# Attention regrouped into two kinds of visits, and a new order of the seven products, in a hybrid Mamba-2 and attention layer

## The chip, the cores and the metric

The kernel runs on one core of one Trainium2 chip. The metric is device time in microseconds of one execution. The reference for the change is the median of three runs of the kernel before. One more execution was recorded by the hardware profiler; every line of a profile below comes from it.

## What is computed

One decoder layer on x of 1024 tokens by 1024 channels, float32. The normed input goes through one large projection (9248 columns), which feeds two branches: a chunked state-space scan (Mamba-2) and a causal attention with 16 heads of 64 and a forgetting term. Both are multiplied by gates, projected, merged, projected once more, normed and added to x. Cut to what matters here:

```python
h = rmsnorm(x, pre_g)
z_ssm, xbc, dt_raw, q, k, v, f_raw, z_att, g_ssm, g_att = split(h @ w_in)
y = ssd(silu(conv(xbc)), softplus(dt_raw + dt_bias), a, d_skip)
y_ssm = group_rmsnorm(y * silu(z_ssm)) * ssm_norm_g
# attention, in blocks of 128 queries, for each head
s = q @ k.T / 8 + fcum[query] - fcum[key]          # fcum = cumsum(log sigmoid(f))
o = softmax(where(key <= query, s, -inf)) @ v
y_att = o * silu(z_att)
merged = sigmoid(g_ssm) * (y_ssm @ w_branch_ssm) + sigmoid(g_att) * (y_att @ w_branch_att)
out = x + rmsnorm(merged @ w_out, post_g)
```

## The kernel before

**Products.** Every large projection is done for a pair of 128-column units at a time (class `Pair`, line 281) by a scheme of Strassen's kind with seven products in place of eight, numbered 1 to 7. A product is 12 matmuls of 128x128 weights by 512 columns: four blocks of the inner dimension, each as high times high, high times low and low times high part, since the operands are split into a rounded part and the rest (`Pair.split` for the weights, tiles `wop`, lines 310 and 311; `Operands.split` for the columns, tiles `x0h`, `x0l` and so on, lines 248 to 252). The product numbers have these column operands: 1 `x0` (b11), 2 `x1` (b21), 6 `x4` (-t2), 5 `x3` (t1), 7 `x5` (t3), 4 `x6` (t4), 3 `x2` (-b22). Products 1, 6, 7 and 4 of a pair add up in one PSUM bank (`pb`). Between two of them ACT copies the sum so far (`keep`, line 358), and the next one must not start before that copy is done. 5 and then 3 use bank `pc`, 2 uses `pd` (or `pc` in attention). `give` (line 361) hands a finished quarter to its consumer, on DVE or, for product 4, ACT. There are 48 pairs.

**The order of the products** is written out by hand in `Stream.__init__` (line 412), as a list of steps. `Stream.half` issues half a product (6 matmuls); the weights of a step are made ready (`prepare`) three steps ahead. Other work is put between half products: `beside` for the scan, `fill` for attention. `halves` (line 533) stops early behind product 7 in attention, because product 4 would have to wait there for the copy of the common bank. Small work for later stages (`chores`: differences of operands on POOL, their stores) is taken off a list, one piece a half product.

**Attention** (from line 1225) runs for 8 pairs of heads, each in 6 groups (`GROUPS`, line 1247). A group is two blocks of 128 queries against up to 512 keys. The loop (line 1542) makes 96 half-visits and 3 more. Each does, in the order of PE's program: `weighted` (weighted sums of v, bank `av`) for what was turned in the half-visit before; `turned` (PE transposes of the exponentials `ex` into banks `pt`, and copies of these to `p` on ACT, line 1429) for half of the group before; `scores` of one query block for two heads (banks `s`, six matmuls on half the rows each, and four small bf16 matmuls `far` on a block that touches the diagonal), then the minimum on DVE (line 1409) and the exp on ACT (line 1412); then half products. Banks `s` and `pt` share four buffers. At the end of two groups, `settle`, `scale` and `send` turn the sums' reciprocals (`tp`, then `st_dram`), `take` loads them back spread over rows (`rb`), `gate` and `out` multiply on POOL, `free` copies `av` to `o` on ACT. Tiles `o` and `zr` have two buffers each.

**Queues.** Each engine does its instructions in order; those marked `pin` keep the program's order, others may be moved by the scheduler. Most DMAs are issued on SP's queue, also in order.

**The end of attention.** The last pair of heads has its output stored to `ya_dram`; its difference t4 is stored too; both are loaded again as `x1l` and `x6l` and split. Products 2 and 4 of the pair `ends[4]` need them. Pair `ends[4]` starts with 5, 6, 7, 2, then 1 of the next pair.

Of the kernel before, what the change touches and what calls it, by code (L numbers as in the profile page):

```python
# [16 lines left out]
P = 128  # L17
# [5 lines left out]
HALF = 512  # L23
# [63 lines left out]
def hybrid_layer(ctx: ExitStack, tc, a, out):  # L87
# [73 lines left out]
    class Operands:  # L161
# [82 lines left out]
        def split(self, name, j):  # L244
            h, l = (t[:, j, :] for t in self.tiles[name])
            raw = l.bitcast(F32)
# [6 lines left out]
            self.left[name].remove(j)  # L253

# [26 lines left out]
    class Pair:  # L281
# [7 lines left out]
        def __init__(self, keys, handlers, ops=None, adds=nc.vector):  # L289
            self.keys, self.handlers = keys, handlers  # L290
            self.ops = xop if ops is None else ops
            self.adds = adds
            self.raw, self.op, self.prepared = {}, {}, set()
            self.s1 = None
# [24 lines left out]
        def prepare(self, which):  # L319
# [15 lines left out]
            elif which == 7:  # L335
                self.split(7, self.total(r["a11"], r["a21"]))
# [38 lines left out]
        def do(self, which):  # L375
            if which in (2, 7, 4, 3):
                unit, ch = {2: (0, 0), 7: (1, 1), 4: (1, 0), 3: (0, 1)}[which]
                for begin in self.handlers[unit][2:]:
                    begin(ch)
            if which == 1:  # L380
                self.b = self.bank.tile([P, HALF], F32, tag="b", bufs=1, name="pb")
                yield from self.matmuls(self.b, 1, "b11", True)
                self.k1 = self.keep(self.b)
            elif which == 2:
                tag = "c" if self.alone else "d"
                ps = pj.tile([P, HALF], F32, tag=tag, bufs=1, name="p" + tag)
# [5 lines left out]
            elif which == 5:  # L392
                self.c = pj.tile([P, HALF], F32, tag="c", bufs=1, name="pc")
                yield from self.matmuls(self.c, 5, "t1", True)
# [10 lines left out]
    class Stream:  # L405
# [6 lines left out]
        def __init__(self, pairs, double, last):  # L412
            self.pairs = pairs
            for n, p in enumerate(pairs):
                p.bank = pjx if n < double and n % 2 else pj
# [18 lines left out]
            self.single = pairs[double : last + 1]  # L434
            for p in pairs:
                p.alone = p in self.single[:-1]
# [788 lines left out]
    with tc.tile_pool(name="att", bufs=1, reuse_waits="tile", side="right") as ap, tc.tile_pool(  # L1225
# [23 lines left out]
        SLOTS = [((2, 3), (0, 1)), ((0, 2), (1, 3)), ((0,), (2,)), ((1, 3), (0, 2)), ((0, 1), (2, 3)), ((0,), (1,))]  # L1249
        ex = ap.tile([P, 2, 4, 256], F32, name="ex")  # L1250
# [21 lines left out]
        class Heads:  # L1272
# [44 lines left out]
            def send(self, n):  # L1317

                tp = pj.tile([P, HALF], F32, tag="d", bufs=1, name="tp")
# [38 lines left out]
            def out(self, n):  # L1358
# [5 lines left out]
                elif self.last:  # L1364
                    nc.vector.tensor_tensor(z, self.av[n], z, ALU.mult)
# [7 lines left out]
        def scores(hp, g, u):  # L1373
# [22 lines left out]
            slots = SLOTS[g][u]  # L1396
            hd = heads[hp]
            for e in range(2):
                def shaped(ap_):
                    return ap_.rearrange("p (a c) -> p a c", c=256) if w == HALF else ap_  # L1400

                if len(slots) == 1:
                    o = ex[:, e, slots[0], 0:w]
                elif w == HALF:
                    o = ex[:, e, slots[0] : slots[1] + 1 : slots[1] - slots[0], :]
                else:
                    o = ex[:, e, slots[0] : slots[1] + 1, :].rearrange("p a c -> p (a c)")[:, 0:w]
# [226 lines left out]
```

## Time and profile before

| what | value |
|---|---|
| median of three runs | 1359.46 us (1355.67 to 1360.33) |
| the profiled execution | 1363.59 us |
| its span, first to last instruction | 1361.8 us |
| granted TensorE clock, mean | 0.993 |
| PE, PEld busy | 96%, 72% of the span |
| DVE, ACT, POOL busy | 72%, 60%, 25% |
| HBM traffic | 170 GB/s over the span |

How to read it: PE is TensorE's matmuls, PEld its loads of weights, which run beside them. DVE is VectorE, ACT ScalarE, POOL GpSimd, SP SyncE. A row of the timeline is: start in us, duration in us, engine, line and operation, output tile and inputs, sizes, and behind "x" how many instructions follow each other; in brackets idle time before it and what ended it. A row of the waits is: who waited for whom, total us, times, longest us. Matmuls are pipelined, their ends are modelled, and a row's duration reaches beyond the start of the next one; the distance between starts is what an instruction takes.

### The profile page before, as it was taken

The page shows a single profiled execution, that of the slowest core. Times are in us where ns is not written, and L with a number is a line of the kernel's source. Part 1 is how long each engine was busy: PE and PEld are TensorE (multiplying, and loading weights), DVE is VectorE, ACT ScalarE, POOL GpSimd, SP SyncE. Part 2 cuts the span into 40 slices and gives each one's busy share as a digit, 9 for nine tenths or more (in the row PEclk, how much of TensorE's full clock was granted, in tenths as well). Part 3 has the DMA queues.
Part 4 walks back from the last instruction along what each step waited for, and adds up shares of the span by engine and source line. Part 5 has one row for each costly group of instructions (what it writes and reads, how often), then busy time and mean ns, then how long its engine had stood idle before and what let it go on. Part 6 is the DMA issues. An engine that isn't in the chain of part 4 may idle for free. (4 is left out here: it accounts for less than half of the span.)

```text
span 1361.8 us, 21004 instructions
## 1 busy us (share of the span) xinstructions
PE 1302.9 (96%) x7070; PEld 980.0 (72%) x7070; DVE 979.0 (72%) x1852; ACT 822.5 (60%) x1773; POOL 336.6 (25%) x270
## 2 busy tenths in 40 slices
PE   5899999999999999999999999999899999889997
PEld 3578888787887888788776666676566665568776
DVE  7979886887878888887665555547655556766975
ACT  7645665566556656565556666668766467633654
POOL 3000440014201420041001223222132322346262
PEclk9999999999999999999999999999999999899989
DMA  7232543445445544444475556468756547576632
GB/s 282 72 108 67 172 133 129 148 151 158 148 142 159 153 138 144 149 134 128 151 244 161 177 178 197 155 213 286 247 179 194 192 144 260 191 235 195 238 102 100
DMA packets 153452, 229.92 MB, mean 169 GB/s; under 512 B 15456, under 2 KB 57920, under 8 KB 153344
## 3 DMA queue, kind: packets, MB, share of 16 engines
q1 hardware_dynamic: 146768, 217.33, 49.7%
q10 hardware_dynamic: 6432, 10.72, 2.1%
q8 instruction: 56, 0.92, 0.3%
q14 instruction: 52, 0.43, 0.1%
q0 software_dynamic: 144, 0.52, 0.1%
HBM read 161.16 MB, written 70.50 MB: 170 GB/s over the span
## 5 line engine op out<-in xcount | busy, mean ns | idle before, releaser
L311 DVE TENSOR_TENSOR wop<-sum,wop 128x512 fp32r<-128x512 f32 x192 | 151.7, 791 | 109.3 <-ACT wop L310 108.9
L310 ACT ACTIVATE wop<-sum 128x512 fp32r<-128x512 f32 x192 | 119.9, 626 | 85.7 <-DVE sum L316 32.1
L1412 ACT ACTIVATE ex<-ex,nm 128x512 f32<-128x512 f32 (+1 forms) x192 | 116.8, 610 | 84.7 <-DVE nm L1409 79.3
L358 ACT ACTIVATE s<-pb 128x512 f32<-128x512 f32 x144 | 85.2, 592 | 99.6 <-PE pb L130 96.5
L130 PE MATMUL pc<-x2h,wop 128*128 128x512 f32 x384 | 132.9, 405 | 6.7 <-DVE th L370 3.2
L130 PE MATMUL pb<-x4h,wop 128*128 128x512 f32 x384 | 130.4, 398 | 1.5 <-ACT x4h L248 1.5
L130 PE MATMUL pb<-x0h,wop 128*128 128x512 f32 x384 | 131.6, 401 | 0.0
L1409 DVE CUSTOM_DVE_ANT_0 ex<-s,fb 128x512 f32<-128x512 f32 (+1 forms) x192 | 99.4, 553 | 44.1 <-PE s L130 43.6
L130 PE MATMUL pc<-x3h,wop 128*128 128x512 f32 x384 | 129.4, 396 | 1.3 <-DVE th L372 1.3
L130 PE MATMUL pb<-x6h,wop 128*128 128x512 f32 x384 | 128.5, 395 | 1.4 <-ACT s L358 1.4
L130 PE MATMUL pb<-x5h,wop 128*128 128x512 f32 x384 | 129.0, 395 | 0.7 <-ACT s L358 0.7
L311 DVE TENSOR_TENSOR wop<-raw,wop 128x512 fp32r<-128x512 f32 x132 | 96.4, 731 | 25.2 <-ACT wop L310 23.5
L133 PE MATMUL pt<-ident,ex 128*128 128x128 f32 x576 | 87.5, 284 | 11.2 <-ACT ex L1412 9.2
L130 PE MATMUL pd<-x1h,wop 128*128 128x512 f32 x288 | 96.9, 395 | 0.6 <-ACT x1h L251 0.6
L310 ACT ACTIVATE wop<-raw 128x512 fp32r<-128x512 f32 x132 | 82.3, 624 | 19.4 <-PE pc L130 11.4
L133 PEld LDWEIGHTS pt<-ident,ex 128*128 128x128 f32 x576 | 61.0, 140 | 45.6 <-issue 20.1
L1429 ACT ACTIVATE p<-pt 128x512 f32<-128x512 f32 (+1 forms) x160 | 81.9, 548 | 18.4 <-PE pt L133 18.3
L130 PEld LDWEIGHTS pc<-x2h,wop 128*128 128x128 f32 x384 | 73.0, 190 | 27.2 <-DVE th L370 4.6
L316 DVE TENSOR_TENSOR sum<-raw 128x512 f32<-128x512 f32 x80 | 61.3, 766 | 42.7 <-DMA raw<-in_wu 31.3
L130 PEld LDWEIGHTS pb<-x4h,wop 128*128 128x128 f32 x384 | 72.9, 190 | 19.3 <-issue 2.0
L130 PEld LDWEIGHTS pb<-x0h,wop 128*128 128x128 f32 x384 | 73.5, 192 | 18.1 <-issue 2.5
L130 PEld LDWEIGHTS pc<-x3h,wop 128*128 128x128 f32 x384 | 72.1, 188 | 19.9 <-issue 2.9
(286 smaller groups left out, 2992.4 us busy)
## 6 DMA issues: line engine op xcount, KB each, us to landing
raw<-in_wu SPq DMA_DIRECT2D x128, 256.0 KB
csb<-cs_dram SPq DMA_DIRECT2D x32, 256.0 KB
fb<-f_dram SPq DMA_DIRECT2D x16, 512.0 KB
rb<-st_dram SPq DMA_DIRECT2D x48, 128.0 KB
wd<-in_wo SPq DMA_DIRECT2D x40, 128.0 KB
xt<-in_x SPq DMA_DIRECT2D x8, 512.0 KB
gs_dram<-th ACTq DMA_DIRECT2D x16, 256.0 KB
qh_dram<-th SPq DMA_DIRECT2D x16, 256.0 KB
```

The source lines that it names most:

```text
L130: return tc.keep_in_program_order(nc.tensor.matmul(*args, **kw))
L133: return tc.keep_in_program_order(nc.tensor.transpose(out_, in_, idn))
L310: nc.scalar.activation(op[:, 0], src, AF.Copy)
L311: nc.vector.tensor_tensor(op[:, 1], src, op[:, 0], ALU.subtract)
L316: self.adds.tensor_tensor(t, x, y, ALU.add)
L358: nc.scalar.activation(s, ps, AF.Copy)
L1409: nc.vector.tensor_tensor_reduce(o, shaped(s[e][:, 0:w]), shaped(fb[hp, h][:, e, 0:w]), 1.0, 3.0e38, ALU.add, ALU.min, nm)
L1412: nc.scalar.activation(o, o, AF.Exp, scale=-1.0, bias=nm, accum_out=hd.at(hd.sm, i, h, e))
L1429: nc.scalar.activation(p[:, :, first:, :], bank[:, :, first:, :], AF.Copy)
```

## The change

Attention now has 48 visits. One does: `weighted` for all that the visit before turned; `scores` for both query blocks of a group; 0.68 of the share of products; `turned` for the whole group, its copies alternately on ACT and DVE; the other 0.32 of the products. The minimum and the exp are pinned. `ex` holds a group in a plain layout. `tp` is put in one of the four score banks. `o` and `zr` have one buffer each, `p` four. Loads are issued at other places of the loop. Where the last outputs of attention are made, `direct` makes the operands b21 and t4 from tiles in the chip's own memory, on DVE and ACT.

The order of the seven products in the main run is 6, 2, 7, 5, 1 of the next pair, 4, 3 (before: 2, 6, 5, 7, with 1 of the next pair behind 7 or, in attention, behind 3). Product 1's bank alternates between two for all pairs, also in attention; the early stop in `halves` is gone. Since 7 may stand before 5, the subtraction of the two follows whichever comes second. Product 7's sum of weights is made in place in the raw tile.

```diff
+        def direct(self, j, outputs, gates, x):
+            pin(nc.vector.tensor_tensor(gates, outputs, gates, ALU.mult))
+            pin(nc.vector.tensor_tensor(x, x, gates, ALU.subtract))
+            for name, raw in (("b21", gates), ("t4", x)):
+                self.at[name, j] = self.step
+                self.split(name, j, raw)
+            self.made.add(("t4", j))
...
             elif which == 7:
-                self.split(7, self.total(r["a11"], r["a21"]))
+                if self.keys[0][0] == "merged":
+                    self.split(7, self.total(r["a11"], r["a21"]))
+                else:
+                    self.adds.tensor_tensor(r["a11"], r["a11"], r["a21"], ALU.add)
+                    self.split(7, r["a11"])
...
-            elif which == 7:
-                yield from self.matmuls(self.b, 7, "t3", False)
-                self.give(1, 1, self.c, self.keep(self.b), "less")
+                else:
+                    yield from self.matmuls(self.b, 7, "t3", False)
+                    self.k7 = self.keep(self.b)
+                self.sums += 1
+                if self.sums == 2:
+                    self.give(1, 1, self.c, self.k7, "less")
...
-                p.bank = pjx if n < double and n % 2 else pj
+                p.bank, p.other = (pj, "be"[n % 2]), (pjx, "d") if n < double else (pj, "c")
...
-                early = [(nxt, 1)] if n + 1 < double else []
-                late = [(nxt, 1)] if n + 1 >= double else []
-                self.steps += [(p, 2), (p, 6), (p, 5), (p, 7)] + early + [(p, 4), (p, 3)] + late
+                self.steps += [(p, 6), (p, 2), (p, 7), (p, 5), (nxt, 1)]
+                self.steps += [(p, 4), (p, 3)] if n + 1 < last else [(p, 3), (p, 4)]
...
-            self.steps += [(a, 5), (a, 6), (a, 7), (a, 2), (b, 1), (a, 4), (a, 3)]
+            self.steps += [(a, 5), (a, 6), (a, 7), (b, 1), (a, 2), (a, 4), (a, 3)]
...
-                if self.run is None and self.at and self.at < len(self.steps):
-                    p, which = self.steps[self.at - 1]
-                    if which == 7 and p in self.single:
-                        return
...
-                tp = pj.tile([P, HALF], F32, tag="d", bufs=1, name="tp")
+                tp = pp.tile([P, HALF], F32, tag="s", bufs=4, name="tp")
...
-                    self.zr = ap.tile([P, HALF], F32, tag="zr", bufs=2, name="zr")
+                    self.zr = ap.tile([P, HALF], F32, tag="zr", bufs=1, name="zr")
...
-                self.o[n] = ap.tile([P, HALF], F32, tag="o", bufs=2, name="o")
+                self.o[n] = ap.tile([P, HALF], F32, tag="o", bufs=1, name="o")
...
-                    nc.vector.tensor_tensor(z, self.av[n], z, ALU.mult)
+                    stream.do_chores()
+                    ops_a.direct(self.hp - KH, self.av[n], z, state["t"])
+                    attended.add((self.hp, 0))
+                    return
...
                 with tc.high_priority():
-                    nc.scalar.activation(p[:, :, first:, :], bank[:, :, first:, :], AF.Copy)
+                    if b % 2:
+                        nc.vector.tensor_copy(to, src)
+                    else:
+                        nc.scalar.activation(to, src, AF.Copy)
...
+        for m in range(6 * NK + 1):
+            last = m == 6 * NK
+            for hd, which in end(m - 2):
+                if (hd.last, which) != (True, 1):
+                    hd.gate(which)
+            for one in made:
+                weighted(*one)
+            for hd, which in end(m - 1):
+                if last:
+                    hd.gate(which)
+                    hd.out(which)
+                    break
+                hd.free(which)
+            if last:
+                break
+            hp, g = divmod(m, 6)
+            if not g:
+                heads[hp] = Heads(hp)
+            for u in range(2):
+                scores(hp, g, u)
+            for hd, which in end(m - 1):
+                (hd.take if (hd.last, which) == (True, 1) else hd.send)(which)
+            for hd, which in end(m):
+                hd.settle(which)
+            loads(m)
+            fill(m, 0.68)
+            for hd, which in end(m - 2):
+                if (hd.last, which) != (True, 1):
+                    hd.out(which)
+            for hd, which in end(m - 1):
+                if (hd.last, which) == (True, 1):
+                    hd.gate(which)
+                    hd.out(which)
+                else:
+                    hd.take(which)
+            for hd, which in end(m):
+                hd.load_gates(which)
+                hd.scale(which)
+            made = turned(hp, g)
+            for hd, which in end(m):
+                if hd.last and which:
+                    hd.send(which)
+            fill(m, 0.32)
+            if m == 6 * NK - 1:
+                heads[hp].take(2)
```

More of the change, by code (lines that the diff above doesn't have):

```diff
@@ L375, in do @@
         def do(self, which):
-            if which in (2, 7, 4, 3):
-                unit, ch = {2: (0, 0), 7: (1, 1), 4: (1, 0), 3: (0, 1)}[which]
+            if which in (2, 4, 3) or which in (5, 7) and self.sums:
+                unit, ch = {2: (0, 0), 4: (1, 0), 3: (0, 1)}.get(which, (1, 1))
                 for begin in self.handlers[unit][2:]:
@@ L1507, in begins @@
                     nc.sync.dma_start(state["t"], ops_a.block("t1", hp - KH))
-            if s == 9 and more:
-                load_v(hp + 1, 1)
-            if s == 10:
+            if g == 4:
                 if more:
@@ L1514, in begins, with end @@
                     state["y"] = fetched("b11", hp - KH)
-        def ended(n):
-            for back in range(6):
-                hp, s = divmod(n - back, 12)
-                if n >= back and hp < NK and s in (3, 7, 11):
-                    yield back, heads[hp], s // 4
+            if g == 5 and more:
+                load_k(hp + 1, 0)
+                load_q(hp + 1, (5, 4))
+        def end(m):
+            hp, g = divmod(m, 6)
+            if 0 <= hp < NK and g % 2:
+                yield heads[hp], g // 2
         load_q(0, (7, 6))
@@ L1532, in hybrid_layer, with fill @@
         weights = (1.1, 1.1, 1.1, 1.1, 0.75, 0.95, 1.05, 0.85)
-        left = [12 * sum(weights) + 3 * weights[-1]]
-        def fill(n):
-            share = weights[min(n // 12, NK - 1)]
+        left = [6 * sum(weights)]
+        def fill(m, part):
+            share = weights[min(m // 6, NK - 1)] * part
             to = stream.steps.index((ends[4], 6))
@@ L1541, in hybrid_layer @@
         made = []
[L1542 to L1572 removed]
+        for m in range(6 * NK + 1):
[13 more added lines that the diff above has]
+                break
+            hp, g = divmod(m, 6)
+            if not g:
[16 more added lines that the diff above has]
+                else:
+                    hd.take(which)
+            for hd, which in end(m):
[4 more added lines that the diff above has]
+                if hd.last and which:
@@ L1583, in hybrid_layer @@
     for n, p in enumerate(ends[4:]):
-        p.bank = pjx if n % 2 else pj
+        p.bank, p.other = ((pjx, "b") if n % 2 else (pj, "b")), (pjx, "d")
     while stream.half():
```

111 lines of the change are left out of this document (34 added, 77 removed).

## The prediction

> **What bounds the kernel now.** I read the page's head first: whose engine is full, and where the granted clock falls.
>
> ```profile
> span 1361.8 us, 21004 instructions
> PE 1302.9 (96%) x7070; PEld 980.0 (72%) x7070; DVE 979.0 (72%) x1852; ACT 822.5 (60%) x1773; POOL 336.6 (25%) x270
> PE   5899999999999999999999999999899999889997
> PEclk9999999999999999999999999999999999899989
> ```
>
> PE is busy in every slice but the first; DVE and ACT have room on the average. The table by stage says the same of each stage (columns: busy time of PE, PEld, DVE, ACT, POOL, then granted clock, DMA share, GB/s); the rows are the scan with its projections, the attention, the few microseconds in which attention ends, and the rest.
>
> ```profile
> 60.00:695.00 635.00, 626.49 (x3211) 506.82 (x3210) 513.09 (x860) 368.71 (x725) 119.72 (x116) 1.00 0.46 144
> 695.00:1179.00 484.00, 469.09 (x2977) 315.05 (x2975) 286.46 (x722) 324.40 (x798) 122.52 (x93) 1.00 0.61 198
> 1179.00:1207.00 28.00, 20.76 (x80) 14.45 (x81) 17.51 (x27) 11.77 (x23) 5.09 (x5) 0.88 0.68 218
> 1207.00:1361.00 154.00, 143.42 (x614) 116.34 (x614) 113.39 (x162) 73.81 (x148) 76.38 (x47) 0.97 0.49 167
> ```
>
> In the 484 us of attention PE idles 14.9 us. So removing waits there can give at most 15 us. But "busy" is not the same as "at its pace", since ends of matmuls are modelled: the distances between starts have to be read. First a product of twelve matmuls in the scan stage, from its first start to the next one's first:
>
> ```profile
> 402.44 0.39 PE L130 MATMUL pd<-x1h,wop 128*128 128x512 f32 x1
> 405.17 0.39 PE L130 MATMUL pb<-x4h,wop 128*128 128x512 f32 x1
> ```
>
> That is 2.73 us, 0.227 us a matmul of 512 columns. Now half-visits of attention, each of which does, in this order, av (weighted sums), pt (turnings), s (scores), products:
>
> ```profile
> 805.57 1.08 PE L130 MATMUL av<-p,v 128*64 128x256 f32 x8
> 806.58 1.09 PE L133 MATMUL pt<-ident,ex 128*128 128x128 f32 x8
> 807.61 0.79 PE L130 MATMUL s<-k,q 64*128 64x384 f32 x6
> ...
> 855.56 0.66 PE L133 MATMUL pt<-ident,ex 128*128 128x128 f32 x4
> 856.15 0.97 PE L130 MATMUL s<-k,q 64*128 64x512 f32 x6
> 857.05 0.50 PE L130 MATMUL pb<-x4h,wop 128*128 128x512 f32 x1
> 859.99 0.65 PE L130 MATMUL av<-p,v 128*64 128x256 f32 x4
> 860.57 0.44 PE L133 MATMUL pt<-ident,ex 128*128 128x128 f32 x2
> ```
>
> Eight turnings take 1.03 us to the next block, four take 0.59: 0.11 each, and 0.15 that does not depend on their number. Eight av matmuls take 1.01, four take 0.58: 0.15 fixed as well. Six score matmuls run as three pairs beside each other (two halves of the rows), 0.68 at the pace above, and take 0.90: 0.22 fixed. The product takes 2.94 instead of 2.73: 0.21 fixed. No wait stands in these rows. So **a half-visit pays 0.73 us for changing the kind of work**, a group of two half-visits 1.46, and 48 groups 70 us. This is the part of the time that the waits don't show.
>
> **The change, part by part.** *Grouping.* The order of PE's instructions in the changed kernel has 48 visits in place of 96: av of a whole group, both blocks of scores, a product part (12 matmuls in 36 visits, 18 in 12), all turnings of the group, 6 more product matmuls. Attention holds 936 product matmuls before and after, and 24 `tp`. Two of the five new boundaries have a row each:
>
> ```profile
> 700.10 0.50 PE L130 MATMUL pc<-x1h,wop 128*128 128x512 f32 x1
> 702.96 1.03 PE L133 MATMUL pt<-ident,ex 128*128 128x128 f32 x8
> ...
> 1188.88 0.44 PE L133 MATMUL pt<-ident,ex 128*128 128x128 f32 x2
> 1189.07 0.48 PE L130 MATMUL pb<-x0h,wop 128*128 128x512 f32 x1
> 1190.64 0.44 PE L130 MATMUL av<-p,v 128*64 128x128 f32 x4
> ```
>
> A product between scores and turnings: 2.86, 0.13 fixed. Turnings ahead of a product: two in 0.19 where the pace says 0.22, so -0.03. A half product between turnings and av: 1.57 against 1.36, 0.21 fixed. Scores ahead of a product: 0.22 as above. Av straight ahead of scores occurs nowhere in the trace; between nothing and the two fixed costs that it replaces (0.30) I take 0.15, that of av ahead of turnings, its nearest row. Sum 0.68 a group: 0.78 saved, times 48 = **-37 us**. Bounds: 45 saved with av to scores free; 18 if that costs 0.30 and the other four cost what their kinds cost above (0.21+0.15+0.21+0.22).
>
> *Second block of scores behind the first one's corner.* Where the block touches the diagonal (32 visits), bf16 corner matmuls now stand between two blocks of scores. Not in the trace: nothing to 0.15 each (the smallest fixed cost), 0 to 5 us. I take **+2**.
>
> *Waits at the turnings.* Most of PE's waits in attention are there already (the list from 695 to 1183: total, times, longest), and behind them stands the chain of DVE and ACT after one block of scores:
>
> ```profile
> PE pt L133 <- ACT ex L1412: 9.2, 14, 3.7
> PE pt L133 <- DVE nm L1409: 1.5, 1, 1.5
> ...
> 857.15 0.69 DVE L1409 CUSTOM_DVE_ANT_0 ex<-s,fb 128x512 f32<-128x512 f32 x1 [1.14 <-PE s L130]
> 857.88 0.72 ACT L1412 ACTIVATE ex<-ex,nm 128x512 f32<-128x512 f32 x1 [0.84 <-DVE nm L1409]
> 858.61 0.71 ACT L1412 ACTIVATE ex<-ex,nm 128x512 f32<-128x512 f32 x1
> 862.42 0.68 DVE L1409 CUSTOM_DVE_ANT_0 ex<-s,fb 128x512 f32<-128x512 f32 x1
> ```
>
> Scores began at 856.15: the minimum starts 1.00 later, the first exp 1.73, the next one 0.73 after that. Four exps, now pinned behind each other, end 4.65 us after the scores begin. PE in that time: two blocks of scores 1.58, a product 2.86, so turnings at 4.44, and the third, the first that reads the fourth exp, at 4.66. The cover is exactly enough where 12 matmuls stand before the turnings (36 visits), and 1.4 us too long where 18 do. Every delay of DVE or ACT ahead of the minima is then a wait of PE: the minimum at 862.42 starts 1.48 behind its scores (860.94, on PE), 0.48 late. I take 0.55 in 36 visits, 20 us, against the 15 that PE idles in the stage now: **+5**. Bounds: none, -15; one DVE and one ACT instruction in front each time (0.69 + 0.59, the copies below), 46 us, +31.
>
> *Turnings evacuated by two engines.* Eighty copies go from ACT to DVE, at about 0.69 us (a DVE subtraction out of the same banks):
>
> ```profile
> L1429 ACT ACTIVATE p<-pt 128x512 f32<-128x512 f32 x127 | 70.8, 591 | 14.7 <-PE pt L133 14.6
> L370 DVE TENSOR_TENSOR th<-pc,s 128x512 f32<-128x512 f32 x11 | 7.6, 692 | 20.0 <-ACT s L358 11.4 <-issue 8.6
> ```
>
> DVE in attention goes from 286 to about 340 us of 447, ACT from 324 to 277. The cover is the six product matmuls (1.57) between turnings and av; nothing counted beyond the delays above.
>
> *Product order and banks.* In the scan, PE idles 8.5 of 635 us; both orders leave a product between each copy of a bank and its next use, and weights are prepared three steps ahead as before. In attention the bank of product 1 now alternates, and 7 is no longer followed by 4 in one bank. Cost **0**, bounds -4 to +4 (half of the idle time there). `tp` in a score bank waits for the first minimum, which starts 1.0 us after the scores and ends at 1.7; `tp` stands at 1.58 or later: within the delays above.
>
> *The end of attention.* The waits from 1179 to 1210, and the clock behind the longest:
>
> ```profile
> PE tp L133 <- DVE ns L1307: 3.2, 1, 3.2
> PE pb L130 <- ACT x4h L248: 1.5, 1, 1.5
> PE pb L130 <- DVE x4l L249: 1.0, 1, 1.0
> PE pd L130 <- ACT x1h L251: 0.6, 1, 0.6
> ...
> 1183.11 0.37 PE L133 MATMUL tp<-ident,ns 128*8 128x128 f32 x1 [3.23 <-DVE ns L1307]
> 1183.71 0.63 PE L130 MATMUL pc<-x2l,wop 128*128 128x512 f32 x1
> 1184.14 1.06 PE L130 MATMUL pc<-x2h,wop 128*128 128x512 f32 x2
> ```
>
> After 3.23 us of idling, matmuls start 0.43 apart instead of 0.23, and the stage's granted clock is 0.88. The change sends the last sums behind the turnings, and `direct` makes the last operands of products 2 and 4 without a trip through memory, with product 1 of the next pair as cover. The waits of t2's parts (x4) stay. Of 6.3 us of waits and some 2 us of slow clock I take **-5**; bounds -9 and +3.
>
> **Sum:** -37 +2 +5 -5 = -35 us. The profiled execution took 1363.6 (span 1361.8); the median of the runs shown is 1359.5, 4.1 less. 1363.6 - 35 - 4.1 = **1324**.
>
> **The rivals.**
>
> *Waits eat the gain.* If the delay is 1.2 us in 36 visits (43 us): -37+2+28-5 = -12, so 1347. For it: no slack in the chain. Against: DVE and ACT now have one gap of several microseconds to catch up in, instead of two short ones.
>
> *Cover was generous.* No waits at the turnings and none at the end: -37-15-9 = -61, so 1298.
>
> *Slower: one buffer for `o` and `zr`.* ACT's copy of av into `o` now waits for POOL's last read of the one before. Now that takes:
>
> ```profile
> 829.64 0.27 PE L133 MATMUL tp<-ident,ns 128*8 128x128 f32 x1
> 838.13 1.28 POOL L1367 TENSOR_TENSOR zr<-o,zr 128x512 f32<-128x512 f32 x1
> ```
>
> From `tp` to POOL's end 9.8 us. In the changed kernel the next copy of `o` is two visits behind, 18 us or more at 9.3 us a visit. SP, too, stands at the load of `zr` until the output before it is stored, and `rb` is queued behind. If this makes POOL over 9 us later, ACT stops with the exps behind it, 23 times: at 3 us each 69 us, and -35+69 = +34, 1393; it is slower from 1.5 us each on. Against it: those 9 us of slack.
>
> *Slower through the clock.* If waits at the turnings pass the 3.2 us after which the pace halved, each costs about 2 us more (some ten matmuls at 0.20 each), 5.2 together, in place of the 0.55 in the sum. Ten such visits give -35+47 = +12, 1371; it is slower from eight on. The Trainium skill, "TensorE: Matmul & The Clock Gate", Parts 1 and 4, has a rule against this change: the clock halves after an idle window of about 3.4 us, and transposes do not count as activity in the same way. By that rule sixteen turnings in a row (1.8 us) plus a wait of 1.6 would do, three times the delay that I take; the trace so far has granted 1.00 in attention, with turnings in every half-visit.
>
> *It does not do what it says.* If the fixed costs move to the new boundaries at full price (18 saved), the second blocks cost 5, and DVE, at 76%, is late by 0.9 in 36 visits (32 us, +17): -18+5+17-5 = -1, 1358, no change.
>
> **How the numbers follow.** Chances: forecast 0.60 (own range 1308 to 1340), waits eat the gain 0.17, generous 0.08, `o` and `zr` 0.07, clock 0.03, not what it says 0.05. A measurement of this kernel can tell about 0.3%, 4 us. Faster: 0.60+0.17+0.08 = 0.85; same 0.05; slower 0.07+0.03 = 0.10. The range goes from 1304 (between forecast and generous) to 1354, which takes in the first rival and leaves out the last three and half of the generous one, some 0.19.
>
> **What would show it.** Steps: starts of av and of the block behind it, 1.0 us for eight and for sixteen about 1.9, must show one fixed cost a block; the stage from 695 to the last av (1191) shrinks from 496 to some 463; PE's waits for ACT's exp at the turnings near 20 us. Wrong if: those waits exceed 40 us, ACT's `o` waits for POOL, the granted clock in attention falls below 0.97, or the scan stage (60 to 695) gets longer by over 4 us.

## The result, and the profile after

The changed kernel takes 1374.59 us in the median of five runs (1368.88 to 1376.63), the kernel before 1360.33 beside it: ratio **1.0102, 95% interval 1.0071 to 1.0134**. It is 1% slower; 1324 was forecast, 35 us faster. The profiled execution took 1368.88, the shortest of the five, so its parts add up to some 5 us less than a usual run.

The head of the page after:

```profile
span 1367.2 us, 20913 instructions
...
PE 1278.0 (93%) x7070; PEld 996.2 (73%) x7070; DVE 1018.3 (74%) x1932; ACT 787.1 (58%) x1693; POOL 340.9 (25%) x270
...
PE   6899999999999999999999989999789997899997
```

PE is busy 25 us less than before and the whole is longer, so PE now waits where it was full. The stages, with the first and the last of attention's matmuls as borders (columns: busy time of PE, PEld, DVE, ACT, POOL, then granted clock, DMA share, GB/s):

```profile
60.00:710.00 650.00, 634.60 (x3232) 513.39 (x3231) 513.30 (x863) 371.91 (x728) 124.82 (x116) 0.99 0.44 140
710.00:1190.00 480.00, 436.74 (x2925) 324.33 (x2924) 317.10 (x791) 284.00 (x709) 121.85 (x94) 0.97 0.59 197
```

In attention PE now idles 43 of 480 us where it idled 15 of 484, and the granted clock is 0.97 where it was 1.00. From the starts of the instructions in both traces (waits are gaps of over 0.3 us on PE; at half clock half of the time is lost):

| | before | after |
|---|---|---|
| the scan's last product starts (no. 201 of 203 or 204) | 685.0 | 699.6 |
| first scores to last av | 495.8 | 492.1 |
| last av to the end | 170.7 | 164.5 |
| waits of PE: scan, attention | 7.7, 15.5 | 15.0, 41.4 |
| time at half clock: scan, attention | 0, 10.2 | 6.8, 27.3 |

One product of 2.7 us has moved from behind attention to ahead of it. So the scan lost 14.6 us where nothing was forecast; attention gained 3.7 instead of 33; its end gained 3.5 besides the moved product.

**The saving itself came.** One visit of the timeline, without waits:

```profile
750.07 0.48 PE L130 MATMUL pc<-x2h,wop 128*128 128x512 f32 x1
...
752.90 1.69 PE L133 MATMUL pt<-ident,ex 128*128 128x128 f32 x14
754.34 0.48 PE L130 MATMUL pb<-x4h,wop 128*128 128x512 f32 x1
...
755.91 1.74 PE L130 MATMUL av<-p,v 128*64 128x256 f32 x16
757.58 0.62 PE L130 MATMUL s<-k,q 64*128 64x256 f32 x6
```

From start to start: a product 2.83 (forecast 2.86), fourteen turnings 1.44, a half product 1.57 (as forecast), sixteen av, four of them with half the columns, 1.67: one fixed cost a block. If each kind of block is counted at the lower quartile of its times, the blocks of attention sum up to 470.8 us before and 436.3 after: **-34.5 us**, forecast -37 and +2. What lies above that sum was 25 us before and is 56 after, and eats the gain. It is in the waits (attention after; total, times, longest):

```profile
PE tp L133 <- DVE nm L1414: 21.0, 11, 4.5
PE pt L133 <- ACT ex L1418: 12.2, 12, 4.2
PE av L130 <- ACT p L1437: 4.6, 5, 1.5
PE tp L133 <- DVE ns L1325: 3.2, 1, 3.2
PE av L130 <- DVE p L1435: 2.2, 4, 1.5
```

The largest is not at the turnings, but at `tp`: it stands right behind the scores and takes the score bank that the first minimum must free. The longest of these places, PE first and then DVE:

```profile
1132.48 0.96 PE L130 MATMUL s<-k,q 64*128 64x512 f32 x6
...
1138.74 0.38 PE L133 MATMUL tp<-ident,ns 128*8 128x128 f32 x1 [4.47 <-DVE nm L1414]
1138.77 0.78 PE L130 MATMUL pc<-x2h,wop 128*128 128x512 f32 x1
1139.35 0.63 PE L130 MATMUL pc<-x2l,wop 128*128 128x512 f32 x1
```

```profile
1133.20 1.77 DVE L321 TENSOR_TENSOR wop<-raw,wop 128x512 fp32r<-128x512 f32 x1
1136.38 0.69 DVE L253 TENSOR_TENSOR x0l<-x0l,x0h 128x512 fp32r<-128x512 f32 x1 [1.42 <-ACT x0h L252]
1137.39 0.69 DVE L253 TENSOR_TENSOR x0l<-x0l,x0h 128x512 fp32r<-128x512 f32 x1 [0.31 <-ACT x0h L252]
1138.00 0.68 DVE L1414 CUSTOM_DVE_ANT_0 ex<-s,fb 128x512 f32<-128x512 f32 x1
```

The minimum could start 1.1 us after the scores, as in undisturbed visits, and starts 5.5 after them. Ahead of it in DVE's order stand a split of weights stretched to 1.77 us (.69 undisturbed) and two splits of operands that wait for ACT. Behind the wait the first two matmuls start 0.58 apart, where the pace is 0.23. In the 48 visits, 12 first minima start 1.9 us or more after their scores. Lateness as such is not new: in the kernel before, 21 of the 96 half-visits have such a first minimum, the longest 5.4 us behind its scores, and PE's waits at the turnings are 10.7 us in all; 15 are of the first block of a group, with the second half-visit, some 5 us, still between it and its turnings. What the change took away is that distance.

### The profile page after: what moved, and what is told of

The parts are those of the page before. It is cut to its first block, busy times and chain, and to the rows that moved or that the text cites. A ratio compares the mean times of both kernels' runs of the same rounds, so it can differ in the third digit from the quotient of the medians.

```text
span 1367.2 us, 20913 instructions
## 1 busy us (share of the span) xinstructions
PE 1278.0 (93%) x7070; PEld 996.2 (73%) x7070; DVE 1018.3 (74%) x1932; ACT 787.1 (58%) x1693; POOL 340.9 (25%) x270
## 5 line engine op out<-in xcount | busy, mean ns | idle before, releaser
L321 DVE TENSOR_TENSOR wop<-raw,wop 128x512 fp32r<-128x512 f32 x176 | 134.2, 763 | 39.1 <-ACT wop L320 38.6
L321 DVE TENSOR_TENSOR wop<-sum,wop 128x512 fp32r<-128x512 f32 x148 | 112.7, 762 | 53.2 <-ACT wop L320 52.8
L130 PE MATMUL pb<-x5h,wop 128*128 128x512 f32 x384 | 133.1, 405 | 3.1 <-ACT s L373 3.0
L320 ACT ACTIVATE wop<-sum 128x512 fp32r<-128x512 f32 x148 | 92.4, 626 | 66.0 <-PE pc L130 28.1
L1414 DVE CUSTOM_DVE_ANT_0 ex<-s,fb 128x512 f32<-128x512 f32 (+1 forms) x192 | 95.8, 552 | 46.2 <-PE s L130 46.2
L320 ACT ACTIVATE wop<-raw 128x512 fp32r<-128x512 f32 x176 | 109.4, 623 | 32.2 <-PE pd L130 21.7
L130 PEld LDWEIGHTS pb<-x5h,wop 128*128 128x128 f32 x384 | 74.2, 193 | 20.3 <-ACT s L373 4.8
L133 PE MATMUL pt<-ident,ex 128*128 128x128 f32 x576 | 76.9, 282 | 12.2 <-ACT ex L1418 12.2
L209 POOL TENSOR_TENSOR wd<-wd 128x256 f32<-128x256 f32 x32 | 33.2, 1038 | 209.4 <-DMA wd<-in_wo 193.9
L130 PEld LDWEIGHTS pb<-x4h,wop 128*128 128x128 f32 x384 | 72.8, 190 | 17.1 <-issue 1.5
L133 PEld LDWEIGHTS pt<-ident,ex 128*128 128x128 f32 x576 | 67.7, 145 | 23.6 <-ACT ex L1418 16.7
```

Of the source, the lines that this page charges most:

```text
L130: return tc.keep_in_program_order(nc.tensor.matmul(*args, **kw))
L133: return tc.keep_in_program_order(nc.tensor.transpose(out_, in_, idn))
L209: pin(nc.gpsimd.tensor_tensor(t[out_], t[a_], t[b_], ALU.subtract))
L320: nc.scalar.activation(op[:, 0], src, AF.Copy)
L321: nc.vector.tensor_tensor(op[:, 1], src, op[:, 0], ALU.subtract)
L1414: nc.vector.tensor_tensor_reduce(o, s[e][:, 0:w], fb[hp, h][:, e, 0:w], 1.0, 3.0e38, ALU.add, ALU.min, nm)
```

## The experiments

Theory A: attention's saving is real, but its cover (what PE does between scores and what needs them) has no slack, and DVE is late; waits and the clock behind them take it back. Theory B: the new order of the seven products costs the scan 12 to 15 us. Times are told as ratios to the kernel before on the same chip; .001 is 1.4 us. Beside each ratio is its interval.

### The scan: order and sum in place

**e1_old_scan_order** puts the scan's order back:

```diff
-                self.steps += [(p, 6), (p, 2), (p, 7), (p, 5), (nxt, 1)]
+                if n + 1 < double:
+                    self.steps += [(p, 2), (p, 6), (p, 5), (p, 7), (nxt, 1)]
+                else:
+                    self.steps += [(p, 6), (p, 2), (p, 7), (p, 5), (nxt, 1)]
```

> The changed kernel, with only the products of the scan stage put back to their order before (2, 6, 5, 7, next 1, 4, 3); attention as changed. In the changed kernel's profile the scan stage ends 14.6 us later than before with the same products. Theory B (the new order itself makes the scan's vectors late: operands that are due sooner, sums that come in another place): the scan stage gives 11 to 15 us back, about 1362 us beside 1375. Rival (the scan is late by the banks that now alternate, or by chance of where vector work falls, whatever the order): within 4 us of 1375, scan stage ends at 697 or later. By theory B attention, 492 us from the first scores to the last output product, stays within 6 us of that.

Measured 1.0065 (1.0041 to 1.0089), 5 us less than the change. The scan's last product starts at 690.5: 9 us are back, 5.5 are not. Neither theory's number; and the interval overlaps that of the change, so that the whole time alone does not show the gain.

**e2_before_new_order** is the opposite, the kernel before with the new order in the scan; since 7 then precedes 5, three sums would be alive at once in two buffers, so the sum for 7 is in place here too.

> The kernel before, with only the products of the scan stage in the new order (6, 2, 7, 5, next 1, 4, 3), the sum for product 7 formed in place as the change does, and the difference given after the second of 7 and 5. Theory B: the scan stage ends 10 to 15 us later than the 685 us of before, some 1372 us in all. Rival (the order is harmless, something else of the change lengthens the scan): within 4 us of 1360.

Measured 1.0187 (1.0159 to 1.0216), +25 us: the scan ends at 703.3 (+18), attention takes 6 more. The parts that concern the products cost more than the whole change does.

**e10_own_sum** is e1, and the sum for product 7 has its own buffer again wherever the order is the old one:

```diff
-                if self.keys[0][0] == "merged":
+                if self.keys[0][0] == "merged" or not self.inplace:
                     self.split(7, self.total(r["a11"], r["a21"]))
```

> The changed kernel with the scan's products in the order before (as in the run of that name, 1368.7 us), and there the sum for product 7 formed in a buffer of its own again, as before. In that run the scan still ended 5.5 us later than before, 1.9 us of it by product 6 and 3.2 at 160 us. If the sum in place is the cause (it holds a weights' buffer until the split, so the next weights come later): the scan gives 4 to 6 us back, 1363 to 1365. If the banks, or the place where products fall, are the cause: within 2 us of 1368.7.

Measured .9998 (.9978 to 1.0018): the scan's last product starts at 682.3, and all that the scan had lost is back, by the profiles 9 us through the order and 8 through the sum in place (by the ratios 5 and 9). The two together are sure, their shares less so: in the nine kernels profiled here that have the scan of the change, the first scores start at 707.0 to 714.7, in the six with the scan of e10 at 691.8 to 695.2. Not all of it reached the end in the profile: e10's attention takes 506.4 us there, 14 more than after, with 49.2 of waits and 44.4 at half clock, in an execution 3.7 us above its median. A place where the sum in place shows, e1's DVE first and then e10's:

```profile
162.82 0.69 DVE L326 TENSOR_TENSOR sum<-raw 128x512 f32<-128x512 f32 x1 [4.44 <-DMA raw<-in_wv]
163.43 0.68 DVE L806 TENSOR_TENSOR m<-m,cbm 128x512 f32<-128x512 f32 x1
```

```profile
156.47 1.10 DVE L807 TENSOR_TENSOR m<-m,cbm 128x512 f32<-128x512 f32 x1
159.33 0.69 DVE L326 TENSOR_TENSOR sum<-raw 128x512 f32<-128x512 f32 x1 [1.75 <-DMA raw<-in_wv]
```

In e1 the next pair's sum stands ahead of the scan's mask `m` on DVE and waits 4.44 us for weights; PE waits 1.99 for `m`, and runs at half clock after it. In e10 the sum stands behind `m`. So two things differ here, when the load lands and where the sum stands in DVE's order; their shares of the 8 us were not separated. Who holds back the weights' loads is seen on SP's queue, after and then before:

```profile
SPq L313 <- DVE wop L321: 50.9, 23, 7.8
...
SPq L313 <- DVE raw L350: 17.2, 6, 6.5
```

```profile
SPq L303 <- DVE sum L316: 31.3, 10, 5.1
SPq L303 <- DVE sum L332: 25.4, 8, 8.4
```

Before, these loads wait for `sum`, which frees a weights' buffer; now they wait for the split or for the sum in place, which come later. In e10 they wait for `sum` again (30.3 and 25.7 us). What the order itself does, beyond more waits of PE for POOL and ACT in the scan, was not taken apart.

### Attention: where is the cause of the waits

**e3_tp_later** moves `send` from behind the scores to behind the first part of the products, and `take` behind the turnings.

> The changed kernel, with only the transpose of the scales (tp) moved from right behind the scores to behind the first part of the products, and the loads of its rows moved behind the turnings. In the changed kernel PE stands 21 us in 11 places at tp, because its bank is one of the scores' four, free only when the first minimum has read it. Theory A1 (the bank's place is the cause; behind one or two products the minimum is long done): those 21 us go, and with them about half of the half-clock time behind the waits, so -18 to -25 us, about 1353. Theory A2 (VectorE is late there, and the late minimum delays the turnings by as much): the waits at the turnings grow from 12 us by nearly the 21, and the time stays within 4 us of 1375.

Measured 1.0050 (1.0027 to 1.0072), -7 us. The waits moved to the turnings, with less at `tp`:

```profile
PE pt L133 <- ACT ex L1418: 20.2, 20, 3.4
...
PE tp L133 <- DVE nm L1414: 6.3, 4, 3.0
```

So the bank of `tp` is where the lateness is met, and only a small part of its cost.

**e8_rb_pool** loads `rb` from POOL's queue:

```diff
-                nc.sync.dma_start(rb[rows[e], :], st_dram...
+                nc.gpsimd.dma_start(rb[rows[e], :], st_dram...
```

> The changed kernel, with only the rows of scales (rb) loaded from GpSimd's queue instead of SyncE's. SyncE's queue stands some 2.8 us at each of these loads, waiting for the scales to be stored, and the weights' loads stand behind it: at 803 us a sum on VectorE waits 2.97 us for such a weight, and PE then 4.2. If late weights behind the rows of scales are the main reason for VectorE's lateness: the waits of 3 us and more fall by half, -12 to -18 us, about 1360. If it is VectorE's own backlog (splits of operands, slowed beside GpSimd): only the wait at 803 goes, -3 to -6 us, about 1370; GpSimd's products start at most 2 us later, which nobody waits for.

Measured 1.0119 (1.0095 to 1.0142), no better. Even at the visit of 792 us, where DVE waited for weights behind `rb`, the minimum is 6.0 us behind the scores instead of 7.2: the weights are late behind other loads as well. That theory falls.

**e5_cover85** gives 85% of the products to the part ahead of the turnings (`fill(m, 0.85)`, then `fill(m, 0.15)`).

> The changed kernel, with 85 % of a block's products between the scores and the turnings and 15 % behind the turnings (68 and 32 in the change). The cover ahead of the turnings grows from 3.0 to 3.8 us on average, that of the copies shrinks from 1.4 to .7. If the waits at the turnings come from a cover too short by what it now gains: their 12 us go, and 5 us of half clock; the waits at tp, 21 us, stay; the outputs wait for copies in some 24 blocks without a product, 0.7 us each, +17. Sum about 0, 1370 to 1380. If copies are quick enough without the products, 1358 to 1362.

Measured 1.0221 (1.0189 to 1.0254), worse than expected. The waits at the turnings went, and the copies lost more:

```profile
PE av L130 <- ACT p L1437: 20.3, 15, 6.4
PE av L130 <- DVE p L1435: 18.7, 20, 2.0
PE tp L133 <- DVE nm L1414: 13.4, 7, 4.0
...
PE pt L133 <- ACT ex L1418: 1.2, 4, 0.3
```

**e6_copies_act** has the copies `p` all on ACT again.

> The changed kernel, with only the copies of the turned probabilities all on ScalarE again, as before (VectorE loses 78 copies of .4 to .7 us, some 50 of its 374 us in attention; ScalarE gains them). The late first minima stand in the same eight blocks of attention in each kernel so far, most of them behind a row of splits on VectorE, which is 69 % busy between 950 and 1070 us, 59 % before. If VectorE's load is the cause: the waits at tp and at the turnings lose 10 to 20 us of 44, and 1358 to 1366 us come out. If the cause is the order in which splits stand ahead of the minimum, not the load: the same blocks are late by the same 2 to 4 us, and ScalarE's copies delay the outputs' matmuls; 1372 to 1385.

Measured 1.0004 (.9975 to 1.0032), -13 us, inside what was expected if DVE's load is the cause. The profile does not show it in the waits, where it had been expected: 22.0 us at `tp` and 10.4 at the turnings, nearly as after. Attention takes 486.4 and its end 162.7, together 7.5 less. The time is the one of the theory, but its path is not shown: 11 first minima are late where after has 12, and in the profile the scan, which this edit does not touch, is 4 us longer. The same edit on e10 (e12 below) takes 13.0 us off attention, 6.4 in waits and half of 13.7 at half clock; why the waits shrink stays open.

**e11_splits_held** lets no splits of operands go in the products ahead of the scores, and up to three at a time behind them.

> The changed kernel, with the splits of the gated operands (x0l to x6l) held back in the second part of a block's products, the part ahead of the scores, and up to three of them let go in the first part, behind the scores. If splits that stand ahead of the first minimum are the cause of VectorE's lateness: the waits in the blocks where they stand (950 to 1190 us) lose a third to a half, 8 to 15 us of 44, about 1362. If something else is (work on weights, GpSimd beside VectorE), within 4 us of 1375.

Measured 1.0176 (1.0149 to 1.0203), 10 us worse. Mostly the same visits are late (12 of now 14); other work of DVE stands ahead of the minimum, and a split comes 4.3 us late for its product at 1228 us. Moving the work about on DVE in this way helps nothing; the next two runs make it less.

**e14_no_gating** leaves out POOL's gating; its outputs are the gates.

> The changed kernel with the gating of attention's outputs on GpSimd left out (its products with the scales and the gates and their sum, 76 us of GpSimd's 124 us in attention; the outputs are then the gates themselves). It tells whether VectorE's late minima come from GpSimd's work beside it, under which VectorE's operations of .68 us take 1.2 to 1.8. If so, half or more of the waits at tp and at the turnings go, -15 to -25 us, 1350 to 1360. If VectorE's own rows of work ahead of the minimum are the cause: -3 to -6 us, 1369 to 1372.

Measured .9989 (.9976 to 1.0002), -15 us. **e15_low_parts_act** forms the low parts on ACT, without the subtraction:

```diff
-                pin(nc.vector.tensor_tensor(l, raw, h, ALU.subtract))
+                pin(nc.scalar.activation(l, raw, AF.Copy))
```

> The changed kernel with the low parts of the operands (x0l to x6l) formed on ScalarE instead of VectorE, which means without the subtraction (the low part is then the whole value; the same number of matmuls and loads). VectorE loses 44 splits, 36 us, between 950 and 1202 us, where they stand right ahead of the late minima; ScalarE gains them. If those splits are what makes the minima late: attention behind 950 us loses 10 to 18 us, 1357 to 1365. If lateness then comes as late exponentials on ScalarE, or if the splits only fill time in which VectorE waits anyway: within 4 us of 1375.

Measured .9965 (.9942 to .9987), -19 us. Each takes about a third off the waits at `tp` or more, and fewer first minima are late, 7 and 9 of 48 where 12 were (e15's waits at the turnings grow by 3); first e14, then e15:

```profile
PE tp L133 <- DVE nm L1413: 14.4, 11, 4.7
PE pt L133 <- ACT ex L1417: 11.0, 7, 3.6
```

```profile
PE pt L133 <- ACT ex L1424: 15.0, 14, 4.2
PE tp L133 <- DVE nm L1420: 12.6, 10, 2.9
```

So DVE is late both by its own row of work and by POOL beside it.

### Do the parts add up

**e12_scan_before_copies_act** is e10 with e6's copies; **e13_e12_tp_later** is that with e3's place of `tp`.

> The changed kernel with two parts undone together: the scan's products in their order before with the sum for product 7 in its own buffer (alone 14 us less than the change, ratio .9998 to before), and all copies of turned probabilities on ScalarE (alone 13 us less, 1.0004). If the two parts lie in different stages and add up: .990 of before, 1347 to 1352, with attention of some 487 to 495 us. If a scan that ends sooner only lets attention meet its waits (the profile of the first had attention 10 us longer): .997 to 1.000.

> The kernel of the run e12, with the transpose of the scales moved behind the first part of the products as well (alone it gave 6 us of the change). If that adds up too: 6 us less than e12, .986 of before. If the late minimum is only met at the turnings instead once the rest is undone: within 2 us of e12.

Measured .9907 (.9887 to .9926), as the sum said, and .9911 (.9888 to .9934). e12 is 13 us faster than the kernel before, e13 no better. But e12's attention still takes 493.4 us, with 42.8 us of waits and 30.7 at half clock.

**e16_scores_first** exchanges two blocks of a visit; av then lies between the scores and what waits for them, with as many changes of kind:

```diff
-            for one in made:
-                weighted(*one)
...
             for u in range(2):
                 scores(hp, g, u)
+            for one in made:
+                weighted(*one)
```

> The changed kernel, with scores and outputs of a visit exchanged: the scores of a group first, then the outputs of the group before, then products, then the turnings. The number of changes between kinds of work stays; the outputs (.8 to 1.9 us) come to lie between the scores and whatever waits for them. If the cover that is too short is the cause of the lost gain: the waits at tp fall from 21 to about 10 us, those at the turnings from 12 to 5, and half of the 13 us lost at half clock goes, -18 to -25 us, about 1352. If VectorE's lateness grows with the earlier start (it has the same work in less time), or the other neighbours cost more per change: within 5 us of 1375.

Measured 1.0011 (.9985 to 1.0037), -12 us, half of what was expected: the waits at `tp` are 14.3, those at the turnings 11.4.

**e17_e12_scores_first** is e12 with this exchange, **e18_e12_no_gating** e12 without gating (its outputs are the gates), **e19_e17_no_gating** e17 without it.

> The kernel of the run e12 (1351 us) with the same exchange of scores and outputs. If cover is what is left: attention falls from 493 to some 475 us, 1330 to 1336, .976 to .980 of before. If not: within 4 us of 1351.

> The kernel of the run e12 (1351 us) with the gating of attention's outputs on GpSimd left out (the outputs are then the gates themselves). If late minima are what keeps attention from the predicted saving: the three reliefs found so far add up, 15 us less than e12, 1335 to 1338. If VectorE has slack there once the copies are gone: within 4 us of 1351.

> The kernel of the run e17 with the gating of attention's outputs left out as well (the outputs are then the gates themselves): both more cover and less lateness. The sum of the blocks at their shortest is 436 us in the change; if waits and half clock are all that lies above it, attention comes to 445 to 460 us and the whole to 1310 to 1325. If something else holds it (weights late, outputs waiting for copies), attention stays above 470 and the whole above 1330.

Measured .9767 (.9742 to .9793), .9768 (.9738 to .9799) and .9682 (.9652 to .9713). **e17 leaves nothing out and takes 1333.35 us beside 1364.65 of the kernel before, 31 us less.** More cover alone and less lateness alone give the same 19 us on e12; both give 31. That these are the two levers shows in the minima: 12 first ones start 1.9 us or more behind their scores in e12, 14 in e17, where only the cover grew, and 6 in e18. First e17's waits in attention and its stage, then e19's waits:

```profile
PE tp L133 <- DVE nm L1418: 14.4, 6, 5.2
PE pt L133 <- ACT ex L1422: 7.5, 12, 2.8
```

```profile
693.00:1165.00 472.00, 442.73 (x3005) 331.65 (x3005) 296.36 (x733) 322.49 (x807) 123.47 (x95) 0.98 0.64 208
```

```profile
PE tp L133 <- DVE nm L1417: 10.1, 5, 7.8
...
PE pt L133 <- ACT ex L1421: 3.9, 9, 1.0
```

| | attention | blocks at lower quartile | waits | at half clock |
|---|---|---|---|---|
| before | 495.8 | 470.8 | 15.5 | 10.2 |
| after | 492.1 | 436.3 | 41.4 | 27.3 |
| e12 | 493.4 | 435.8 | 42.8 | 30.7 |
| e17 | 472.1 | 432.4 | 27.4 | 17.1 |
| e18 | 472.2 | 433.5 | 29.4 | 17.1 |
| e19 | 461.1 | 432.6 | 18.8 | 10.2 |

The blocks stay at 432 to 436 us in every kernel with the new visits. Blocks, waits and half of the time at half clock add up to attention's time within 5 us in every row. With waits and half clock near those of before (e19, which leaves the gating out), attention comes to 461, where the prediction had put it (463). That is theory A, shown.

## Why the prediction was wrong

*Grouping, -37 and the second block of scores, +2:* right, -34.5 together. Where the changes of kind stood in the profile before, their price held.

*Waits at the turnings, +5:* **this step failed.** It took .55 us in 36 visits, 20 in all, as an average delay of a chain that had no slack. The waits of attention came to 41, 26 more than before, and not as a small delay everywhere: 12 first minima start 2.0 to 7.2 us behind their scores and the others 1.8 at most, where 1.1 is undisturbed, behind rows of splits and sums. The prediction read one late minimum (.48 us); the 21 of the trace before, up to 5.4 us, could have been read there. The first of the rivals, "waits eat the gain", had the mechanism and took 43 us for the waits, about what they are; but it counted no half clock.

*`tp` in a score bank, "within the delays above":* failed in that the largest row of waits stands there, though e3 shows that most of it would be met at the turnings anyway.

*Two engines for the turned copies, 0:* failed. e6 puts it at -13 us without them; it does not show by which path.

*Product order and banks in the scan, 0 (±4):* **failed**, +14.6. "Weights are prepared three steps ahead as before" looked at when they are issued in the program. It left out when a weights' buffer comes free and where the sum then stands in DVE's order, which the sum in place changes (8 us of it), and how the new order places DVE's and POOL's work against the scan's own (some 9 us, cause not taken apart). The two together cost e2 25 us. The profiled execution's span came out 5 us longer where 35 less were forecast, 40 apart; the scan's 15 and the 26 by which what lies above the blocks grew beyond the forecast (31 in place of 5) make that up.

*The end of attention, -5:* nearly right, -3.5 beside the product that moved. PE's waits behind 1190 us are 1.9 us, where 7.5 stood from 1179 to 1212. But sending the last pair's sums straight behind the turnings brought a new wait one sum earlier, the 3.2 us of `tp` for `ns` above (at 1180.73), which counts with attention's.

*The clock, a rival at .03:* partly right. Attention's time at half clock grew from 10.2 to 27.3 us, so 9 us were lost; it was to need eight to ten visits of over 3.2 us, and came with six stretches. Shorter waits are enough, see below. *One buffer for `o` and `zr`:* did not happen; ACT's copy of av waits for PE alone:

```profile
ACT o L1366 <- PE av L130: 19.4, 17, 3.0
```

Of the signs that the prediction named as proof against it, the scan longer by over 4 us came, the clock stands on the line (0.97), and the waits pass 40 us only with those at `tp`.

## What to carry to other kernels

When PE's order is regrouped, price the changes of kind by the starts of instructions; that part holds. Then do not average the chain that must fit under the cover: look at each of its places, at what stands ahead of its first instruction on that engine, in bursts and beside POOL, and give the cover slack; here an exchange of two blocks (av behind the scores) gave it for nothing. A sum in place cost 8 us here, and the loads in the queue then waited for other instructions: check who releases a buffer before costing such an edit at zero.

## What the hardware did that was not expected

*The clock halves after waits of 2 us, but not after each.* In the scan after, PE waits twice and then falls to half pace; the second view is the table by stretches, its seventh column the granted clock:

```profile
318.80 0.39 PE L130 MATMUL pd<-x1h,wop 128*128 128x512 f32 x1
321.52 0.50 PE L130 MATMUL pb<-x5h,wop 128*128 128x512 f32 x1 [2.33 <-ACT s L373]
...
322.56 0.51 PE L130 MATMUL pb<-x5l,wop 128*128 128x512 f32 x1
322.87 1.05 PE L130 MATMUL pb<-x5h,wop 128*128 128x512 f32 x2
```

```profile
317.00:322.70 5.70, 3.37 (x15) 2.46 (x14) 2.84 (x7) 3.50 (x10) 0.62 (x1) 1.00 0.84 304
322.70:326.10 3.40, 3.40 (x10) 2.62 (x9) 2.49 (x5) 3.19 (x9) 1.74 (x2) 0.50 0.21 77
448.00:452.40 4.40, 2.36 (x10) 1.42 (x8) 3.29 (x6) 3.66 (x9) 3.76 (x1) 1.00 0.62 235
452.40:455.80 3.40, 3.40 (x17) 2.83 (x17) 1.96 (x5) 0.22 (x2) 0.43 (x1) 0.50 0.20 77
```

The waits are 2.33 and 2.04 us, and the half pace lasts 3.41 us each time (6.83 in three of the ten places during the run). Yet a wait of 1.94 us (to 429.85) and one of 3.18 (to 1180.73) in the same trace have no slow stretch behind them. All changes of the granted clock in the 18 profiles of this document lie on steps of 3.413 us. Counted by these steps, from 65 us on and at full clock, the next step ran at half pace in all 115 cases in which PE idled 2.0 us or more within one, in none of 6307 with under 1.2 us, and in 39 of the 166 between. So the idle time within one step counts, not the length of a wait alone (what tips it between 1.2 and 2.0 us stays open): the waits of 1.94 and 3.18 us were each divided between two steps, .58 and 1.36, 1.87 and 1.31. The prediction took 3.2 us as the least wait, from one place, but the trace before shows less: half pace began there at 1181.11, 1.2 us into that wait, and at 1297.17 it came behind a wait of 1.85 us. The Trainium skill, "TensorE: Matmul & The Clock Gate", Part 1, "What's actually happening", gives a window of 3413 ns; the lengths agree. Its rule in "HAM oscillation", no idle gaps of over about 3.4 us, is too lenient here: 2.33 and 2.04 us were enough.

*DVE is slow beside POOL mainly where it reads two tiles of SBUF.* In attention after, at least 21 of DVE's instructions with two inputs in SBUF (splits and sums of 512 columns, .67 to .69 us alone) took 1 to 1.78 us. None of the 192 minima, 80 copies and 34 results that read PSUM took more than .692, though 77 of them ran beside POOL. An exception is `ns<-sm` (line 1317), 8 columns times a number, with one input in SBUF: .17 us alone, .73 to 1.24 in five of its eight places, each time until .03 us behind the end of a POOL instruction. Three splits of one operand, two of them stretched, ahead of a minimum, and POOL beside them:

```profile
1158.04 4.03 DVE L250 SCALAR_TENSOR_TENSOR x4l<-x4l,x4h 128x512 fp32r<-128x512 f32 x3
1161.99 0.41 DVE L1414 CUSTOM_DVE_ANT_0 ex<-s,fb 128x256 f32<-128x256 f32 x1
```

```profile
1157.60 1.65 POOL L326 TENSOR_TENSOR sum<-sum,raw 128x512 f32<-128x512 f32 x1 [7.06 <-DVE wop L321]
1159.33 1.59 POOL L350 TENSOR_TENSOR raw<-raw 128x512 f32<-128x512 f32 x1
```

The Trainium skill says this of the two engines in "SBUF — State Buffer", "Who interferes with whom": a VectorE instruction with two inputs in SBUF contends with a GpSimd instruction that reads SBUF, one with at most one does not, unless it runs in a mode with two ports, which `tensor_scalar` is said to be able to enter. The trace agrees: the splits and sums are of the first kind, and `ns<-sm` is a `tensor_scalar`.
